# A row scale spread over the partitions through DRAM, and a first tile loaded in two halves, in a one-core encoder layer

## The chip, the cores and the metric

The kernel runs as one program on one core of a Trainium2 chip. The metric is the device time of an execution in microseconds. The profile is one execution taken by the hardware profiler; its engines are PE (TensorE matmul), PEld (TensorE weight loads), DVE (VectorE), ACT (ScalarE), POOL (GpSimd) and SP (SyncE, which issues most of the DMAs).

## The reference, cut to what matters

One layer of an encoder with two groups of heads side by side, on a prompt of 2048 tokens and a sample of 256, both with the same weights; then a gated MLP with a depthwise convolution over positions, and a final norm.

```python
def rmsnorm(x, w):
    y = x * lax.rsqrt(jnp.mean(x * x, axis=-1, keepdims=True) + EPS)
    return y * w

def encoder_layer(x, ...):
    h = rmsnorm(x, norm1_w)
    p = h @ w_in                                   # mLSTM q,k,v,o and gates; attention q,k,v
    mq, mk, mv, mo, gates, aq, ak, av = jnp.split(p, cuts, axis=-1)
    m_out = mlstm_mixer(mq, mk, mv, mo, gates, b_gates, mh_norm_w)   # both directions
    a_out = attention_mixer(aq, ak, av, q_norm_w, k_norm_w)          # 8 heads, 2 kv heads, rotary
    x = x + jnp.concatenate([m_out, a_out], axis=-1) @ w_out
    h = rmsnorm(x, norm2_w)
    u = centred_dwconv(h @ w_up, conv_w, conv_b)   # width 3 over positions
    a, g = jnp.split(u, 2, axis=-1)
    return x + (jax.nn.silu(g) * a) @ w_down
# then rmsnorm(x, final_norm_w); D_MODEL 1024, D_FF 2816, all float32
```

The change touches two places of this: the loading of the first tile of `x` for `h @ w_in`, and the scale `rsqrt(mean + EPS)` of the second norm, for one block of 256 tokens.

## The kernel before, in words

The 2304 tokens are 18 tiles of 128 (`NT`) or 9 blocks of 256 (`NB`, `BT`). Activations are kept transposed: the feature is the partition, tokens lie along the free dimension, and the 1024 features are eight chunks (`NCC`). Float32 products are made of three matmuls: each operand is split into a rounded part and the rest (`hi`, `lo`; ScalarE makes the first with a copy, VectorE the second with a subtraction), and hi·hi, hi·lo and lo·hi are added in PSUM.

The phases are: A, the norm-free projection of attention's columns and the gates; then the mLSTM and attention side by side (`run_both`); C, the output projection with the residual and the second norm; D, the MLP.

**Phase A's launch.** `front(i)` loads tile `i` of transposed `x` (512 KB, `g.xA[i]`) on SP's queue, and splits it into `nT`. `weights(cs)` loads chunk `c` of the weights (400 KB, `g.w_a[c]`) and splits it, scaled by the norm's weight, into `ws[c]` (helper `split`, L104 to L109). `mm` multiplies: the first call takes tiles 16 and 17 together, chunk by chunk, so that its first matmuls need only chunk 0 of the tile and of the weights. The program order is: tile 16 (the first of `order`), chunks 0 and 1 of the weights, tile 17, the other six chunks, tile 0, then the norms and the rotary tables (`tables`, `tables2`). `post1` turns a projected tile into q, k, v and gates, and frees one of three PSUM buffers `pj`.

**Phase C's tail.** Phase C goes over the nine blocks in the order `ORDER`, whose last is block 7. For each block `mm` (L989) projects into four PSUM tiles `po`; `post` adds the residual (L996), stores the new `x` to `x1_d` and squares it (L999); `tail` adds the squares up, gets the scale from `rstd_bc`, multiplies the four tiles `cx` by it and by the norm's weight (L1014, eight instructions) and stores them to `n2_d` (L1016; on POOL's queue for the last block, on SP's otherwise).

`rstd_bc` sums over partitions with matmuls against a matrix of ones (L128). The result is a column per 128 tokens: the token is the partition. From it comes the scale, for the last block (`act=True`) by a square root on ScalarE (L133), VectorE's reciprocal (L138) and a correction step in three VectorE instructions (L139 to L141), for all others by a power on POOL (L143). The multiplication in `tail` wants it the other way, along the free dimension and the same in every partition. L145 does that: for each 128 tokens a matmul whose stationary operand is the column repeated 128 times and whose moving operand is the identity. Its result stays in the same PSUM tile, `rs_c`.

For the last block the tail is called by `g.c_end()`, after the first two pairs of phase D's up-projection have been begun (tiles `pa`, `pb`) and their weight sums made (`sums`, L1110). Then phase C's pools are closed and phase D's opened over the same memory: the conv input tiles `u` (tag `u` of pool `d_s`, six buffers), the PSUM tiles `pc`, the conv outputs `y`, and three activation operands (`LATE`). The first `u` buffer lies over the bytes of phase C's `sq` and `rcol` buffers, another four over tiles of `cmx` that have been read out; the second `pc` bank is the bank of `rs_c`.

**Phase D** goes over three token blocks of 768 and eleven groups of the hidden dimension; each pair of 128 hidden columns is a Strassen-like product of seven multiplications (`11`, `21`, `t2`, `t1`, `t3`, `22`, `t4`) that share the banks `p1` (`pa`), `p2` (`pb`) and `p3` (`pc`). A step copies a bank to `u` on ScalarE (L1156) or adds it on VectorE (L1159) and then lets the next multiplication add into the bank (L1152). So the `t2` product of a pair, into `pa`, waits for the copy of `pa` into `u`; the `t1` product, into `pc`, waits for no copy.

**The order on each engine** is not the program's: a planner places instructions by priority, which is the place in the program (moved up within `tc.high_priority`), and by a simulation of when each is ready. It gives memory of closed pools to new tiles once the last users of the old ones are placed, and adds the waits that this needs, tile by tile. Each engine then executes its own list strictly in order.

Of the kernel before, what the change touches and what calls it, by code (L numbers as in the profile page):

```python
# [9 lines left out]
F32 = mybir.dt.float32  # L10
F32R = mybir.dt.float32r
AF = mybir.ActivationFunctionType
ALU = mybir.AluOpType
# [4 lines left out]
P = 128  # L18
D = 1024
NCC = D // P  # L20
# [65 lines left out]
def f32(ap):  # L86
    return ap.bitcast(F32)
# [14 lines left out]
def split(g, hi, lo, src, r, col=None):  # L102
    nc = g.nc
    nc.sync.dma_start(r, src)  # L104
    nc.scalar.activation(hi, r, AF.Copy, scale=1.0 if col is None else col)  # L105
    if col is None:
        nc.vector.tensor_tensor(lo, r, f32(hi), ALU.subtract)
    else:
        nc.vector.scalar_tensor_tensor(lo, r, col, f32(hi), ALU.mult, ALU.subtract)  # L109
# [10 lines left out]
def rstd_bc(g, sp, pp, sqs, n, ptag, name, bufs=1, act=False):  # L120


    nc = g.nc
    k = n // P
    ps = pp.tile([P, 512], F32, tag=ptag, name="rs_" + name, bufs=bufs)
    for t in range(k):
        for i, sq in enumerate(sqs):
            nc.tensor.matmul(ps[:, 504 + 2 * t:506 + 2 * t], sq[:, t * P:(t + 1) * P], g.ones, start=i == 0,  # L128
                             stop=i == len(sqs) - 1)
    r = sp.tile([P, 4], F32, tag="rcol", name="rcol_" + name)[:, 0:k]  # L130
    if act:
        sr = sp.tile([P, 4], F32, tag="rcol0", name="rcol0_" + name, bufs=1)[:, 0:k]
        nc.scalar.activation(sr, ps[:, 504:504 + 2 * k].rearrange("p (t o) -> p t o", o=2)[:, :, 0], AF.Sqrt, bias=g.eps)  # L133
    nc.vector.tensor_scalar(r, ps[:, 504:504 + 2 * k].rearrange("p (t o) -> p t o", o=2)[:, :, 0], EPS, None, ALU.add)
    if act:
        v, r = r, sr
        u = sp.tile([P, 4], F32, tag="rcol1", name="rcol1_" + name, bufs=1)[:, 0:k]
        nc.vector.reciprocal(r, r)  # L138
        nc.vector.scalar_tensor_tensor(u, r, -0.5, r, ALU.mult, ALU.mult)  # L139
        nc.vector.tensor_tensor(u, u, v, ALU.mult)  # L140
        nc.vector.scalar_tensor_tensor(r, u, 1.5, r, ALU.add, ALU.mult)  # L141
    else:
        nc.gpsimd.tensor_tensor(r, r, g.mhalf[:, 0:k], ALU.pow)  # L143
    for t in range(k):
        nc.tensor.matmul(ps[:, t * P:(t + 1) * P], r[:, t:t + 1].to_broadcast([P, P]), g.ident, start=True, stop=True)  # L145
    return ps[:, 0:n]


def phase_a(g, tc, sw, st_x, after_x, after_mm, after_pj):


    nc = g.nc
    with ExitStack() as st:
        sp = st.enter_context(tc.tile_pool(name="a_s", bufs=2, reuse_waits="tile"))
# [23 lines left out]
        def front(i):  # L178
            b, o = i // 2, i % 2
            nT = nTs[i] = sf.tile([P, NCC, 2, P], F32R, tag="nT", name=f"n1T{i}", bufs=3)  # L180
            n = order.index(i)
            x = xw[n] if n < NX0 else sx.tile([P, NCC, P], F32, tag="x", name=f"x{i}", bufs=3)
            nc.sync.dma_start(x, g.xA[i])
            nc.scalar.activation(nT[:, :, 0, :], x, AF.Copy)
            nc.vector.tensor_tensor(nT[:, :, 1, :], x, f32(nT[:, :, 0, :]), ALU.subtract)

        def norm(i):
            b, o = i // 2, i % 2
# [10 lines left out]
        def weights(cs):  # L199
            for c in cs:  # L200
                r = first[NX0 + c] if NX0 + c < 8 else sx.tile([P, D], F32, tag="x", name=f"ra{c}", bufs=3)
                split(g, ws[c][:, 0, :], ws[c][:, 1, :], g.w_a[c], r[:, 0:800], g.n1w[:, c:c + 1])
# [111 lines left out]
        def post2(i, kz):  # L314
# [5 lines left out]
            nc.scalar.dma_start(g.k_d[:, :, i * P:(i + 1) * P].rearrange("g p t -> p g t"), f32(kT))  # L320

        front(order[0])
        weights(range(0, 2))
        front(order[1])
        weights(range(2, NCC))
        front(order[2])
        for i in order[0:2]:
            norm(i)
# [616 lines left out]
def phase_c(g, sn, sp, pp, wps):  # L945
# [59 lines left out]
    def tail(b, x, acc):  # L1005
        if b == ORDER[-1]:
            sqs = [acc[:, 0], acc[:, 1], g.last_sq[:, 0], g.last_sq[:, 1]]
        else:
            nc.vector.tensor_tensor(acc[:, 0], acc[:, 0], acc[:, 1], ALU.add)
            sqs = [acc[:, 0]]  # L1010
        r = rstd_bc(g, sp, pp, sqs, BT, "r", f"c{b}", act=b == ORDER[-1])
        for z in range(4):
            for o in range(2):
                nc.vector.scalar_tensor_tensor(x[z][:, o], x[z][:, o], g.n2w[:, 2 * z + o:2 * z + o + 1],  # L1014
                                               r, ALU.mult, ALU.mult)
            (nc.gpsimd if b == ORDER[-1] else g.st).dma_start(g.n2_d[:, 2 * z:2 * z + 2, b * BT:(b + 1) * BT], x[z])  # L1016
        g.normed.add(b)
# [309 lines left out]
def down_phase(g, tc, st, s1, sl, banks):  # L1327
# [45 lines left out]
    def finish(accs, b, z, sms, bank):  # L1373
        r = rstd_bc(g, sp, bank, sms, H, "p", f"d{b}_{z}", bufs=4)

        def out(c):
            a = accs[c][:, Z[z]]
            if (b, z) == (ND - 1, 0) and c >= HALF:
                nc.vector.scalar_tensor_tensor(a, a, g.fw[:, c:c + 1], r, ALU.mult, ALU.mult)
            else:  # L1380
                nc.vector.tensor_tensor(a, a, r, ALU.mult)
            g.st.dma_start(g.yT[c, :, b * BLK + z * H:b * BLK + (z + 1) * H], a)
        for c in range(NCC):
            out(c)
# [55 lines left out]
def body(tc, aps, phases="abcd"):  # L1440
    nc = tc.nc
    g = Ctx()
# [3 lines left out]
    with ExitStack() as st:  # L1446
# [6 lines left out]
        def dram(name, shape):  # L1453
            setattr(g, name, dp.tile(shape, F32, name=name))
# [9 lines left out]
        dram("k_d", [2, P, T])  # L1464
        dram("v_d", [2, P, NT, 2, HD])
        dram("nm_d", [NT, 17, P])
        dram("og_d", [4, NB, P, 2, P])
        g.ident = kp.tile([P, P], F32, name="ident")
        make_identity(nc, g.ident)
# [12 lines left out]
        with ExitStack() as s2:  # L1482
# [8 lines left out]
            with ExitStack() as s3:  # L1491
                rp = pool(s3, "rowp", bufs=1)
                g.rows = rp.tile([40, 2, T], F32, name="rows")
                g.lnr = rp.tile([P, NT], F32, name="lnr")
                g.gtm = rp.tile([P, NT, 2, 16], F32, name="gtm")

                def after_x():
                    g.sn = pool(s_wo, "m_n", bufs=1, side="right")

                def after_mm():  # L1500
                    g.sm = pool(s_m, "m_s", bufs=2, side="right")

                def after_pj():
                    g.pj = pool(s_m, "m_j", bufs=MJ, space=PSUM, side="right")

                phase_a(g, tc, sw, s3.enter_context(ExitStack()), after_x, after_mm, after_pj)
                gate_math(g, tc)
# [143 lines left out]
```

## Time and profile before

| what | us |
|---|---|
| median of 3 runs (lowest, highest) | 3327.17 (3326.01, 3334.67) |
| the profiled execution | 3327.39 |
| its span, first to last instruction | 3325.7 |
| TensorE busy in the span | 3238.2 (97%) |
| VectorE busy | 2429.5 (73%) |
| ScalarE busy | 2002.8 (60%) |
| GpSimd busy | 519.0 (16%) |
| mean DMA rate | 184 GB/s |

Phase A takes the first 200 us or so, phase C's own blocks lie between about 1430 and 1850 us beside attention's last part, and phase D fills the rest. Line numbers in the profile (L145) are those of the kernel's file. A wait is shown as idle time before an instruction and, behind an arrow, the instruction whose semaphore ended it. Matmuls are pipelined: a matmul's duration is longer than the distance to the next, so the time of a row of matmuls is to be read from starts.

### The profile page before, as it was taken

Reading aid. Unit: us, or ns where it says so; the run is one execution under the profiler, and the core shown is the slowest. Engines: PE = TensorE matmul, PEld = TensorE weight load, DVE = VectorE, ACT = ScalarE, POOL = GpSimd, SP = SyncE. Lnnn points to the kernel's source line nnn. Section 1 sums busy time; section 2 is a strip of 40 time slices with the busy share of each in tenths; the row PEclk is TensorE's granted clock in tenths of the full one; section 3 lists DMA queues with packets and bytes.
Section 4 is the critical chain, followed back from the end, with each engine's and each line's share of the span. In section 5 each row is a group of like instructions: output and inputs, shape, how many; then the busy total and the mean of one; then the engine's idle time right before and its main releaser. Section 6 shows DMA issues by size and latency. Waiting matters only on the chain.

```text
span 3325.7 us, 53327 instructions
## 1 busy us (share of the span) xinstructions
PE 3238.2 (97%) x19488; PEld 3017.3 (91%) x19488; DVE 2429.5 (73%) x3768; ACT 2002.8 (60%) x3765; POOL 519.0 (16%) x916
## 2 busy tenths in 40 slices
PE   8989999999999999999999899999999999999998
PEld 7878888888888878878889899999999999999998
DVE  7855676676657778786665899998888888666664
ACT  5646666666675676665552655666666667554543
POOL 4551033222232322210000000000000000010101
PEclk9999999999999999999999899999999999999999
DMA  9973333332335433533227666668676557967663
GB/s 348 319 207 108 113 113 102 110 108 94 109 114 177 131 110 120 162 100 107 85 89 266 230 240 211 231 231 273 205 266 235 202 199 252 318 229 269 216 238 127
DMA packets 364301, 612.31 MB, mean 184 GB/s; under 512 B 31605, under 2 KB 220455, under 8 KB 364039
## 3 DMA queue, kind: packets, MB, share of 16 engines
q1 hardware_dynamic: 330727, 563.14, 50.4%
q0 software_dynamic: 11856, 33.96, 3.7%
q10 hardware_dynamic: 21456, 11.80, 1.2%
q8 instruction: 154, 2.52, 0.3%
q14 instruction: 108, 0.88, 0.1%
HBM read 444.85 MB, written 163.93 MB: 183 GB/s over the span
## 4 chain that ended last, share of the span: by engine, by line
PE 58%; issue 3%; DVE 2%; DMA 2%; ACT 2%; POOL 1%; SPq 0%; POOLq 0%; DVEq 0%; ACTq 0%
PE pa L1152 17%; PE pc L1152 8%; PE pf L1416 7%; PE po L989 5%; PE pb L1152 4%; PE ph L1416 4%; PE pg L1416 2%; PE ps L582 1%; PE mj L745 1%; PE ps L583 1%; PE pv L599 1%; PE pv L601 1%; PE pv L600 1%; PE px L559 1%; PE mv L745 1%
## 5 line engine op out<-in xcount | busy, mean ns | idle before, releaser
L588 DVE TENSOR_TENSOR xx<-pe,xx 128x1024 fp32r<-128x1024 f32 x260 | 318.8, 1227 | 128.1 <-ACT xx L587 126.5
L561 DVE TENSOR_REDUCE mx<-px 128x1 f32<-128x1024 f32 x256 | 310.8, 1217 | 100.2 <-PE px L559 99.1
L586 ACT ACTIVATE pe<-ps 128x1024 f32<-128x1024 f32 x260 | 266.4, 1025 | 171.0 <-PE ps L583 164.2
L587 ACT ACTIVATE xx<-pe 128x1024 fp32r<-128x1024 f32 x260 | 274.9, 1058 | 5.0
L1369 POOL TENSOR_TENSOR sq<-sq,sq 128x384 f32<-128x384 f32 x38 | 48.8, 1284 | 1377.9 <-ACT sq L1365 1294.9
L989 PEld LDWEIGHTS po<-cmx,wo 128*128 128x128 f32 x1728 | 227.2, 189 | 17.9 <-DVE cx L996 1.2
L989 PE MATMUL po<-cmx,wo 128*128 128x256 f32 x1728 | 234.6, 283 | 1.2 <-DVE cx L996 0.8
L1156 ACT ACTIVATE u<-pa 128x386 f32<-128x386 f32 (+2 forms) x264 | 129.1, 489 | 175.4 <-PE pa L1152 169.4
L601 PE MATMUL pv<-xx,vv 128*128 128x512 f32 x520 | 210.8, 405 | 7.4 <-DVE xx L588 7.3
L599 PE MATMUL pv<-xx,vv 128*128 128x512 f32 x520 | 211.5, 407 | 6.5 <-ACT rs L609 3.2
L582 PE MATMUL ps<-qq,kk 128*128 128x512 f32 x520 | 213.3, 410 | 3.1 <-DVE mx L561 1.5
L583 PE MATMUL ps<-qm,kl 65*128 65x512 f32 x520 | 208.6, 401 | 0.0
L600 PE MATMUL pv<-xx,vl 128*64 128x512 f32 x520 | 206.9, 398 | 0.0
L717 PEld LDWEIGHTS mj<-mn,wm 128*128 128x128 f32 x1296 | 177.6, 192 | 18.4 <-ACT og L733 4.1
L717 PE MATMUL mj<-mn,wm 128*128 128x256 f32 x1296 | 190.2, 287 | 3.3 <-ACT og L733 2.9
L727 PE MATMUL mv<-wm,mn 128*128 128x256 f32 x1296 | 188.6, 286 | 1.3 <-ACT qb L723 1.3
L727 PEld LDWEIGHTS mv<-wm,mn 128*128 128x128 f32 x1296 | 174.6, 190 | 14.0 <-ACT qb L723 2.3
L238 PE MATMUL pj<-w_a,n1T 128*128 128x512 f32 (+1 forms) x864 | 168.5, 354 | 10.0 <-ACT w_a L105 7.1
L238 PEld LDWEIGHTS pj<-w_a,n1T 128*128 128x128 f32 x864 | 141.8, 192 | 29.8 <-ACT w_a L105 7.1
L559 PE MATMUL px<-kk,qq 128*128 128x512 f32 x512 | 165.6, 404 | 2.8 <-ACT pe L586 2.5
L828 ACT ACTIVATE dm<-dm,tm 128x128 f32<-128x128 f32 x288 | 95.6, 392 | 101.1 <-POOL dm L825 97.1
L1152 PE MATMUL pc<-nt,wb 128*128 128x386 f32 (+2 forms) x792 | 147.2, 340 | 0.3 <-DVE cx L1014 0.3
(336 smaller groups left out, 8114.8 us busy)
## 6 DMA issues: line engine op xcount, KB each, us to landing
mn<-n_d SPq DMA_DIRECT2D x216, 256.0 KB, 3.1
ru<-w_up SPq DMA_DIRECT2D x88, 512.0 KB, 5.7
rs<-wsu_d SPq DMA_DIRECT2D x88, 512.0 KB, 5.7
act_d<-ts SPq DMA_DIRECT2D x33, 768.0 KB, 6.1
nt<-act_d SPq DMA_DIRECT2D x60, 384.0 KB, 4.6
re_t<-wsd_d SPq DMA_DIRECT2D x45, 512.0 KB, 5.4
wsu_d<-tw SPq DMA_DIRECT2D x44, 512.0 KB, 4.1
act_d<-ya SPq DMA_DIRECT2D x99, 192.0 KB, 2.9
```

The costliest lines, as they stand in the source:

```text
L238: nc.tensor.matmul(pjs[t][:, c0:c1], nTs[tiles[t]][:, c, a, :], ws[c][:, b, c0:c1], start=(c == 0 and k == 0), stop=(c == NCC - 1 and k == 2))
L561: nc.vector.tensor_reduce(s.mx[:, t0, z0:z0 + 1], ps, AX.X, ALU.max)
L582: nc.tensor.matmul(o, kk[:, kc:kc + P], s.qq, start=True, stop=False)
L586: nc.scalar.activation(pe, ps, AF.Exp)
L587: nc.scalar.activation(x[:, 0], pe, AF.Copy)
L588: nc.vector.tensor_tensor(x[:, 1], pe, f32(x[:, 0]), ALU.subtract)
L599: nc.tensor.matmul(s.pv, vv[:, kt % 4, :], x1, start=kt == 0, stop=False)
L717: nc.tensor.matmul(pj[:, o].rearrange("p (n t) -> p n t", t=P), s.w[c][:, a, o * P:(o + 1) * P], nT[c][:, :, h, :], start=(c + o + k == 0) ...
L727: nc.tensor.matmul(pv[:, o], nT[c][:, o, a, :], s.w[c][:, h, 256:512], start=(c + o + k == 0), stop=(c == NCC - 1 and k == 2 and o == 1))
L989: nc.tensor.matmul(po[:, o], wo[c][z // 2][:, a, n], mx[c][:, h, :], start=c + o + k == 0, stop=c == NCC - 1 and o == 1 and k == 2)
L1152: s.nc.tensor.matmul(p, w[:, aa, c, :], ops[k][:, c, bb, 0:s.n], start=c == 0 and i == 0 and not add, stop=c == NCC // 2 - 1 and i == 2, s ...
L1416: nc.tensor.matmul(ps[c], w[:, aa, c, :], t[:, gi - g0, bb, 0:H], start=gi == 0 and m == 0 and not more, stop=gi == NG - 1 and m == 2, ski ...
```

## The change

In `rstd_bc`, for the last block of phase C alone (`act=True`), the scale `r`, with the token as partition, is written by a DMA on POOL's queue to a small DRAM tensor `rl_d`, element by element in transposed order, and read back by another DMA on the same queue into a new SBUF tile `rb` with the row repeated in all 128 partitions. `rb` uses the one buffer of tag `sq`. The two matmuls of L145 are not issued for this block, and the eight multiplications of `tail` read `rb` from SBUF in place of `rs_c` from PSUM. The other blocks, and the final norm, are as before.

In `front`, the first tile of x is loaded in two DMAs of four chunks each, with a copy and a subtraction for each; the load and split of weight chunk 0 stand between the two halves in program order. `weights` is then called for chunk 1 alone behind it.

```diff
@@ rstd_bc
     else:
         nc.gpsimd.tensor_tensor(r, r, g.mhalf[:, 0:k], ALU.pow)
+    if act:
+        nc.gpsimd.dma_start(g.rl_d.rearrange("t p -> p t"), r)
+        rb = sp.tile([P, k, P], F32, tag="sq", name="rb_" + name, bufs=1)
+        nc.gpsimd.dma_start(rb, g.rl_d[:].unsqueeze(0).to_broadcast([P, k, P]))
+        return rb.rearrange("p t q -> p (t q)")
     for t in range(k):
         nc.tensor.matmul(ps[:, t * P:(t + 1) * P], r[:, t:t + 1].to_broadcast([P, P]), g.ident, start=True, stop=True)
     return ps[:, 0:n]
@@ phase_a, front
-            nc.sync.dma_start(x, g.xA[i])
-            nc.scalar.activation(nT[:, :, 0, :], x, AF.Copy)
-            nc.vector.tensor_tensor(nT[:, :, 1, :], x, f32(nT[:, :, 0, :]), ALU.subtract)
+            for c in (slice(0, NCC // 2), slice(NCC // 2, NCC)) if n == 0 else (slice(0, NCC),):
+                nc.sync.dma_start(x[:, c], g.xA[i, :, c])
+                if c.start == 0 and n == 0:
+                    weights(range(0, 1))
+                nc.scalar.activation(nT[:, c, 0, :], x[:, c], AF.Copy)
+                nc.vector.tensor_tensor(nT[:, c, 1, :], x[:, c], f32(nT[:, c, 0, :]), ALU.subtract)
@@ phase_a
         front(order[0])
-        weights(range(0, 2))
+        weights(range(1, 2))
         front(order[1])
@@ body
+        dram("rl_d", [2, P])
```

## The prediction

> **What bounds the kernel now.** I read the engine shares first, then TensorE's waits over the whole run, then order of time at the two places that the diff touches.
>
> The page's head: engine, busy time and share, instructions.
>
> ```profile
> span 3325.7 us, 53327 instructions
> PE 3238.2 (97%) x19488; PEld 3017.3 (91%) x19488; DVE 2429.5 (73%) x3768; ACT 2002.8 (60%) x3765; POOL 519.0 (16%) x916
> ```
>
> TensorE bounds it: 97% busy. So the question at each place is whether TensorE's idle time there shrinks or grows, and whether anything later takes that back. The view of waits, of 1780 to 1900 us and then from 1850 us to the end (total, times, longest):
>
> ```profile
> PE rs_c L145 <- DVE rcol_c L141: 15.2, 1, 15.2
> ...
> PE rs_d L128 <- POOL sq L1369: 4.5, 2, 4.3
> PE rs_d L145 <- POOL rcol_d L143: 1.2, 1, 1.2
> PE rs_d L128 <- DVE sq L1369: 1.1, 1, 1.1
> ```
>
> The first row is the longest single wait of TensorE that I found in the run, and the change removes the instruction that waits. The other three are all the waiting that follows 1850 us, 6.8 of 1475 us, each behind TensorE's own products: a shift of TensorE at 1850 us reaches the end in full. The timeline around the wait (start, duration, engine, line, operation, count, idle before):
>
> ```profile
> 1811.82 13.79 PE L989 MATMUL po<-cmx,wo 128*128 128x256 f32 x114
> ...
> 1828.03 0.59 PE L128 MATMUL rs_c<-ones,csq 128*128 128x2 f32 x4
> ...
> 1831.51 0.16 DVE L134 TENSOR_SCALAR rcol_c<-rs_c 128x2 f32<-128x2 f32 x1 [0.68 <-ACT rcol_c L133]
> ...
> 1832.25 0.95 DVE L1077 TENSOR_TENSOR nt<-nt 128x772 fp32r<-128x772 f32 x1
> ...
> 1834.93 1.22 DVE L1125 TENSOR_TENSOR wb<-tw,wb 128x1024 fp32r<-128x1024 f32 x1
> ...
> 1843.64 0.15 DVE L141 SCALAR_TENSOR_TENSOR rcol_c<-rcol_c,rcol_c 128x2 f32<-128x2 f32 x1
> 1843.85 1.22 PE L145 MATMUL rs_c<-ident,rcol_c 128*128 128x128 f32 x4 [15.23 <-DVE rcol_c L141]
> ...
> 1844.72 3.44 PE L1152 MATMUL pc<-nt,wb 128*128 128x386 f32 x12
> 1845.11 3.22 DVE L1014 SCALAR_TENSOR_TENSOR cx<-cx,nw,rs_c 128x256 f32<-128x256 f32 x8 [1.31 <-PE rs_c L145]
> 1845.24 0.88 ACT L1156 ACTIVATE u<-pa 128x386 f32<-128x386 f32 x2 [4.90 <-PE rs_c L145]
> ...
> 1848.47 2.34 PE L1152 MATMUL pc<-nt,wb 128*128 128x386 f32 x12 [0.31 <-DVE cx L1014]
> 1848.95 2.96 POOL L1016 DMA_DIRECT2D n_d<-cx  x4 [39.78 <-DVE u L1159]
> ...
> 1850.65 4.40 PE L1152 MATMUL pa<-nt,wb 128*128 128x386 f32 x24
> ```
>
> The reader is to see a chain: sums of squares (L128), four tiny DVE steps that stand between long DVE work and end at 1843.79, the spread (L145), eight multiplications (L1014), and behind them phase D. Two rows show how phase D hangs on it. ScalarE's first copy into `u` (L1156) waits for the spread: the first `u` buffer lies on the bytes of phase C's `sq` and `rcol` buffers, so it waits for their last reader. And the second `pc` product waits for the multiplications, since its PSUM bank is that of `rs_c`. The `pa` products at 1850.65 need that `u` copy, because they add into the bank that it empties.
>
> **The change part by part.** *The tail.* Removed: the two matmuls of L145 (four passes, 1.22 us). TensorE no longer waits for L141. The bank of `rs_c` now has its last reader at L134, over by 1831.67. So the two `pc` products (24 matmuls) follow L128 directly and need only `nt` (1833.20) and `wb`, the last of which is ready at 1836.15: they are done near 1842 even at a slow start. That empties the old place; it isn't yet a gain, for the next product in the order is the first `pa`, and it waits for the `u` copy.
>
> What that copy waits for has become longer. The new tile `rb` takes the one buffer of tag `sq`, under the first `u`; its last readers are the eight multiplications. New on the path are a POOL write of 256 single elements to DRAM and a POOL read of 128 KB that gives every partition the row. Neither shape is in the trace on POOL's queue; the nearest rows (landing times minimum, median, maximum; first POOL stores of `mix_d`, then SP reads of `rb` from `nm_d`, also a row of 256 elements for 128 partitions, then POOL reads of `dm` from `nm_d`, 256 KB to 128 partitions):
>
> ```profile
> L621 POOL DMA_DIRECT2D mix_d<-o x70: 521/550/623, 241.3 to 1723.8; - x70
> DMA to landing us min/median/max: 2.0/2.6/7.2
> ...
> L773 SPq DMA_DIRECT2D rb<-nm_d x9: 359/371/384, 1244.5 to 1402.1; - x9
> DMA to landing us min/median/max: 3.0/3.1/3.4
> ...
> L821 POOL DMA_DIRECT2D dm<-nm_d x72: 536/590/632, 234.9 to 1411.4; - x72
> DMA to landing us min/median/max: 3.3/3.7/6.9
> ```
>
> And how long POOL takes to begin after its data is made:
>
> ```profile
> 1722.27 0.41 DVE L615 TENSOR_TENSOR o<-o,rs 128x256 f32<-128x256 f32 x1
> ...
> 1723.21 1.08 POOL L621 DMA_DIRECT2D mix_d<-o  x2 [20.32 <-ACT xx L587]
> ```
>
> From 1722.68 to 1723.21 are 0.53 us. I take 0.53 + 2.6 for the write and 3.3 for the read: the SP row's 3.1, whose pattern is the same, and 0.2 for POOL's slower issue (590 against 371 ns). That is 6.4 us. The ends are 2.0 + 3.0 = 5.0 and 0.5 + 7.2 + 6.9 = 14.6.
>
> By "DMA: Bandwidth & Descriptors" of the Trainium skill, section on the anatomy of a SWDGE DMA, each such transfer costs about 2.0 us plus its bytes at 436 GB/s. By that, an estimate, the two take 2.0 + 2.3 = 4.3 us and the forecast falls by 2.1 us. The POOL rows here are longer (64 KB in 2.6 against its 2.15 us), so I keep the rows.
>
> Now the sum. The scale is ready at 1843.79 as before: L134 to L141 are untouched, and so is the DVE work between them. Plus 6.4 is 1850.2. The eight multiplications take 3.22 as before: 1853.4; from SBUF they may be a little shorter, at most 0.4 us. One `u` copy, half of 0.88 and a little overlap, is 0.5, and I allow 0.1 for handing over: TensorE starts the `pa` products near 1854.0, against 1850.65: **3.4 us later**.
>
> A second price comes with it. TensorE restarts slowly after a long idle time: twelve `pc` products took 3.44 us at 1844.72 and 2.34 at 1848.47; the four passes of L145 took 1.22 us, and in block 6:
>
> ```profile
> 1811.46 0.61 PE L145 MATMUL rs_c<-ident,rcol_c 128*128 128x128 f32 x4
> ```
>
> Together 1.1 + 0.6 = 1.7 us. Before, this lay under the wait for the multiplications; now TensorE idles from about 1842 to 1854 and pays it on products that the rest waits for. I add **1.7**; the ends are 0 and the 2.0 us that the launch shows below. Delay at the tail: **5.1 us**. The old path from 1843.79 to 1850.65 was 6.9 long, so the low end is 5.0 + 3.2 + 0.5 − 6.9 = 1.8, less 0.4 for SBUF, 1.4; the high end is 14.6 + 3.2 + 0.6 − 6.9 + 2.0 = 13.5.
>
> What else moves: on POOL's queue the four stores of `n2_d` (L1016) stand behind the two new DMAs and go some 5 us later. POOL had been idle for 39.8 us, so nothing else is delayed there; `n2_d` of block 7 is read only for the last third of phase D. The conv outputs' buffers wait for these stores too (L1273), but that work follows the pair's products, which move along by the same 5 us. SP issues the next `ru` loads after the `wd` split on DVE, also 5 us later; their weights are split before 1862.1 and used first at 1867.57:
>
> ```profile
> 1860.81 1.22 DVE L1125 TENSOR_TENSOR wa<-ru,wa 128x1024 fp32r<-128x1024 f32 x1
> ...
> 1867.57 4.42 PE L1152 MATMUL pa<-n,wa 128*128 128x386 f32 x24
> ```
>
> The use moves along, so 5 us of slack stay.
>
> *The launch.* Added: one DMA on SP, one ScalarE copy and one DVE subtraction, the copy and the subtraction each of half size, and the first weights' DMA before the second half of x. The rows:
>
> ```profile
> 5.05 1.06 ACT L184 ACTIVATE n1T<-first 128x1024 fp32r<-128x1024 f32 x1 [2.98 <-DMA first<-xA]
> ...
> 7.14 0.80 PE L238 MATMUL pj<-w_a,n1T 128*128 128x512 f32 x1 [7.14 <-ACT w_a L105]
> ...
> 26.96 1.26 DVE L216 COPY rot<-qkw 128x16 f32<-128x16 f32 x8 [7.78 <-DMA qkw<-q_norm_w]
> ...
> PE pj L238 <- DVE n1T L185: 1.9, 1, 1.9
> PE pj L238 <- DVE t L273: 0.5, 1, 0.5
> ...
> 10.00:15.00 5.00, 5.00 (x18) 4.26 (x17) 4.68 (x6) 4.62 (x6) 0.00 (x0) 1.00 1.03 396
> 15.00:20.00 5.00, 5.00 (x30) 4.42 (x29) 3.85 (x4) 3.67 (x5) 0.47 (x3) 1.00 1.06 395
> ...
> 30.00:35.00 5.00, 5.00 (x26) 4.18 (x25) 5.00 (x13) 3.25 (x5) 5.00 (x12) 1.00 1.02 347
> ```
>
> (The last three are stretches: length, busy time and count of PE, PEld, DVE, ACT, POOL; granted clock; DMA share; GB/s.) The first product can start earlier by at most the half copy (0.53) and the wait for half the tile, 256 KB at the 350 to 396 GB/s of these stretches, 0.7 us; I take 0.8 of these 1.2. But the stretches show TensorE slow at first (18 matmuls against 30 in 5 us, 2.0 us lost), and the two waits, at 38 and 40.6 us, 2.4 us together, end with DVE work. DVE is full from 30 us on, and its run began at 26.96 with a load that no part of the change brings earlier, since the DMA engines are full (share 1.03, 1.06). So TensorE's 0.8 us turn into a longer wait there: **0**, between −1.2 if DVE's order shifts with it and +0.4, one SP issue (371 ns in the row above) ahead of all later loads.
>
> **The rivals.** *The two transfers are slow.* The DMA engines are still full of weight traffic while the scale becomes ready:
>
> ```profile
> 1828.60:1844.00 15.40, 0.17 (x2) 0.15 (x1) 14.51 (x22) 11.33 (x14) 0.00 (x0) 0.55 1.04 369
> 1844.00:1851.00 7.00, 6.69 (x30) 6.39 (x31) 5.36 (x12) 2.56 (x6) 2.05 (x3) 0.78 0.30 105
> ```
>
> The share falls from 1.04 to 0.30 just then, which speaks against it; the 256 single elements, which no row shows, speak for it. At 14.6 us the delay is 11.5 and 1.7 for the restart: about 3340.6. It makes the kernel measurably slower (0.3%, 10 us, about what a measurement of this kernel can tell) once the two take 11.4 us.
>
> The same page of the Trainium skill says in its specifications that transfers under 512 B are done as read-modify-write; its rules call strided elements one descriptor each. By that the write is the suspect. No run here shows it yet.
>
> *TensorE finds other work in the gap.* The second pair's `u` buffers lie under `cmx` tiles that are read out by 1825.6, so that pair's products need not wait. If the planner orders them before the first pair's, TensorE does four more products (2.2 us each, half of 4.40) by 1854: 3.4 − 8.8 + 1.7 = −3.7, about 3323.5. Against it: the rows show both pairs' copies on ScalarE in program order, and phase D's buffers are handed out after the tail is placed.
>
> *The `pc` products stay behind the tail.* Then the old order holds and 4.7 us of work (twice 2.34) moves behind 1854: about 3337. Against it: nothing stands before them on TensorE once L145 is gone.
>
> *Nothing is felt.* Short transfers (5.0) and no slow restart: 1.4 us, with the launch's 1.2 gained, the time of before.
>
> **How the numbers follow.** The sum is made against the profiled execution, 3327.4 us (span 3325.7), which lies 0.2 us from the median of the runs. Plus 5.1 is 3332.5; its own range is 3329 to 3336. Chances: this 0.55; slow transfers 0.13; work in the gap 0.13; `pc` behind 0.05; nothing felt 0.14. A range of 3322 to 3338 leaves out most of the slow transfers and the far end of reordering elsewhere, since a planner that simulates the whole program may place other instructions anew. Over 0.3% slower: most of the slow transfers, some of `pc` behind, 0.14; over 0.3% faster needs nearly the whole 15.2 us, 0.06; within, 0.80.
>
> **What would show it.** Right: L145 gone for `rs_c` of block 7; twenty-four `pc` matmuls before 1843; then a gap of 10 us or more on TensorE that ends with the `u` copy, itself after L1014; the first `pa` 3 to 4 us later than 1850.65 and slow; at the launch an earlier first matmul and a longer wait near 38 to 41 us. Wrong: `pa` products of the second pair inside the gap, an earlier end of L141, or a write that lands after more than 5 us.

## The result: 23 us slower, and the profile after

The changed kernel takes 3351.24 us (median of 4 runs, 3350.45 to 3356.23) against 3328.45 us (4 runs, 3326.01 to 3334.67): a ratio of 1.0065, with a 95% interval of 1.0052 to 1.0077. The forecast was 3332.5 us, at most 3338. The mechanism came as forecast; two terms of its sum were far too small, and the launch wasn't free.

The head of the page after (span; engine, busy time and share, instructions):

```profile
span 3348.7 us, 53329 instructions
PE 3250.4 (97%) x19484; PEld 3026.4 (90%) x19484; DVE 2428.9 (73%) x3769; ACT 2002.8 (60%) x3766; POOL 519.1 (16%) x918
```

TensorE's waits after, from 1850 us to the end (total, times, longest):

```profile
PE pa L1160 <- ACT u L1164: 23.3, 1, 23.3
PE rs_d L128 <- POOL sq L1377: 4.3, 2, 2.8
PE rs_d L150 <- POOL rcol_d L143: 1.2, 1, 1.2
PE rs_d L128 <- DVE sq L1377: 1.1, 1, 1.1
```

The 15.2 us in front of the spread have gone, and 23.3 us in front of the first `pa` product have come. The timeline after, at that place (start, duration, engine, line, operation; line numbers are 5 to 8 higher than before):

```profile
1838.93 0.15 DVE L138 RECIPROCAL rcol_c<-rcol_c 128x2 f32<-128x2 f32 x1
...
1840.48 7.08 PE L1160 MATMUL pc<-nt,wb 128*128 128x386 f32 x24 [3.86 <-ACT wb L1132]
...
1850.98 0.15 DVE L141 SCALAR_TENSOR_TENSOR rcol_c<-rcol_c,rcol_c 128x2 f32<-128x2 f32 x1
1854.10 0.77 POOL L145 DMA_DIRECT2D rl_d<-rcol_c  x1 [37.52 <-issue]
1862.56 0.58 POOL L147 DMA_DIRECT2D rb_c<-rl_d  x1 [7.69 <-DMA rl_d<-rcol_c]
1866.92 3.26 DVE L1022 SCALAR_TENSOR_TENSOR cx<-cx,nw,rb_c 128x256 f32<-128x256 f32 x8 [15.79 <-DMA rb_c<-rl_d]
1868.10 3.11 POOL L1024 DMA_DIRECT2D n_d<-cx  x4 [4.96 <-DVE cx L1022]
1870.34 0.88 ACT L1164 ACTIVATE u<-pa 128x386 f32<-128x386 f32 x2 [22.64 <-DVE cx L1022]
...
1870.88 6.93 PE L1160 MATMUL pa<-nt,wb 128*128 128x386 f32 x24 [23.32 <-ACT u L1164]
```

Read it from the bottom: `pa` waits for the `u` copy, this for the multiplications (L1022), these for the read of `rb`, this for the write of `rl_d`, and this starts 2.97 us after L141 has ended at 1851.13. From L141's end to `pa` are 19.75 us, of which 15.8 lie in the write's start, its landing and the read. The stretch from 1854 to 1863 (length; busy time and count of PE, PEld, DVE, ACT, POOL; granted clock; DMA share; GB/s) shows that nothing competes:

```profile
1854.00:1863.00 9.00, 0.00 (x0) 0.00 (x0) 0.00 (x0) 0.00 (x0) 1.21 (x2) 0.50 0.01 0
```

The whole core stands still for one kilobyte, with the DMA engines at a share of 0.01. The DMA view of 1851 to 1871 us (KB each, us to landing):

```profile
rb_c<-rl_d POOLq DMA_DIRECT2D x1, 128.0 KB, 4.3
rl_d<-rcol_c POOLq DMA_DIRECT2D x1, 1.0 KB, 7.8
```

The difference of the two profiled spans, 23.0 us, splits at two marks. The reciprocal comes 7.3 us later (1838.93 against 1831.59). From there to the first `pa` product are 31.96 us against 19.06, 12.9 more, and from that product to the end 1477.8 against 1475.0, 2.8 more. The first says little of the change: among the experiments below whose launch is that of before, the reciprocal came at 1834.67 (`tail_only`) and at 1840.28 us (`tail_fixed`). The second proved the same wherever the tail is the same: 31.96 in `tail_only`, and 19.07 to 19.17 in three kernels with the tail of before. The third didn't: in `tail_only` the rest took 1474.0 us, less than before.

### The profile page after: what moved, and what is told of

It is laid out like the page before. It is cut to its first block, busy times and chain, and to the rows that moved or that the text cites. A ratio compares the mean times of both kernels' runs of the same rounds, so it can differ in the third digit from the quotient of the medians.

```text
span 3348.7 us, 53329 instructions
## 1 busy us (share of the span) xinstructions
PE 3250.4 (97%) x19484; PEld 3026.4 (90%) x19484; DVE 2428.9 (73%) x3769; ACT 2002.8 (60%) x3766; POOL 519.1 (16%) x918
## 4 chain that ended last, share of the span: by engine, by line
PE 82%; issue 6%; DMA 3%; DVE 3%; ACT 3%; POOL 2%; SPq 1%; POOLq 0%; ACTq 0%; DVEq 0%
PE pa L1160 17%; PE pc L1160 8%; PE pf L1424 7%; PE po L997 5%; PE pb L1160 4%; PE mj L725 4%; PE pj L246 4%; PE ph L1424 4%; PE mv L735 4%; PE ps L590 3%; PE pv L607 3%; PE ps L591 3%; PE pv L609 3%; PE pv L608 3%; PE px L567 3%
## 5 line engine op out<-in xcount | busy, mean ns | idle before, releaser
L246 PE MATMUL pj<-w_a,n1T 128*128 128x512 f32 (+1 forms) x864 | 169.1, 354 | 11.2 <-ACT w_a L105 6.9
L1160 PE MATMUL pa<-nt,wb 128*128 128x386 f32 (+2 forms) x792 | 147.9, 342 | 23.3 <-ACT u L1164 23.3
L1160 PEld LDWEIGHTS pa<-nt,wb 128*128 128x128 f32 x792 | 141.7, 191 | 23.6 <-ACT u L1164 23.6
```

The costliest lines, as they stand in the source:

```text
L246: nc.tensor.matmul(pjs[t][:, c0:c1], nTs[tiles[t]][:, c, a, :], ws[c][:, b, c0:c1], start=(c == 0 and k == 0), stop=(c == NCC - 1 and k == 2))
L1160: s.nc.tensor.matmul(p, w[:, aa, c, :], ops[k][:, c, bb, 0:s.n], start=c == 0 and i == 0 and not add, stop=c == NCC // 2 - 1 and i == 2, s ...
```

## The experiments

Ratios are to the kernel before on the same chip, where its median was 3330.8 to 3331.8. "Tail" is the spread through DRAM, "launch" the first tile's halves and the first weights.

### The two parts, each alone

`front_only`: the diff without its change in `rstd_bc` and without `rl_d`.

> Only the launch part of the change (first tile of x in two halves around the first weights); the tail is that of before. Theory A: the 7.3 us by which block 7's first DVE step (L134, 1831.51 before, 1838.85 after) came later were caused by the launch part, through the other order that the planner then wrote for DVE, ACT and POOL; then this kernel takes about 3327.4 + 5 to 8 = 3332 to 3335 us, and the shift of its TensorE is already 1 to 2 us at 90 us and 4 to 5 us at 1400 us. Rival (the prediction): the earlier start is absorbed at 40 us and nothing else moves: 3326 to 3328 us.

3336.3 us (12 runs), 1.0016 (1.0006 to 1.0026): about 5 us slower (2 to 9 by the interval), where I had forecast nothing. Behind the reciprocal its trace is that of before (1495.0 us to the end against 1494.1). TensorE's waits in its first 200 us, beside those of before (7.1 at first, 1.9 and 0.5 near 40 us, which the prediction shows, and 2.7 in three waits at the product now at L321):

```profile
PE pj L241 <- ACT w_a L105: 7.2, 1, 7.2
PE pj L241 <- ACT xh L251: 4.7, 1, 4.7
PE pk L321 <- DVE kz L286: 3.7, 1, 3.7
```

Single waits have grown and others have gone: all of TensorE's waits in the first 200 us add up to 16.3 us here, 15.0 before and 15.1 in the changed kernel. So they don't carry the 5 us.

`tail_only`: only the change in `rstd_bc`, and `rl_d`.

> Only the tail part (the scale of block 7 through DRAM); the launch is that of before. Theory: parts add up; the tail costs what lies between L134 and the first pa product (19.1 us before, 32.0 after, so 12.9) plus 2.8 behind it: 3343 us, with the same three long steps (POOL starts 3 us late, the write takes about 8 us to land, the read about 4). Rival: the POOL write was slow only because the launch part had shifted the weights' traffic against it; then it lands in 2.6 us as the prediction took, and the kernel takes about 3333 us.

3347.96 us (4 runs), 1.0052 (1.0034 to 1.0069). The order of all instructions is that of before up to the tail. From the reciprocal to the first `pa` are again 31.96 us. So the tail makes about 17 of the 23 us and the launch about 5; 0.52% and 0.16% make 0.68%, and 0.65% was measured for both.

### Which queue, and the buffer under `u`

`tail_sp`, and `tail_clear`, each against the tail alone:

```
tail_sp:    - nc.gpsimd.dma_start(g.rl_d..., r)    + nc.sync.dma_start(g.rl_d..., r)
            - nc.gpsimd.dma_start(rb, ...)         + nc.sync.dma_start(rb, ...)
tail_clear: - tag="sq", bufs=1 (rb), tag="rcol0", bufs=1 (root)   + tag="mx", bufs=MXB (both)
```

> As tail_only, but both new DMAs are issued on SP's queue. Theory W: the write of 256 single 4-byte elements to one KB of DRAM is slow whoever issues it; only POOL's late start (3.0 us) and its slower issue go, so the write still takes 6 us or more to land: about 3339 us. Rival Q: POOL's software queue made it slow; then the write lands in 2.2 us and the read in 3.1 as SP's other rows show, and the kernel takes about 3332 us.

3345.04 us, 1.0038 (1.0023 to 1.0053). SP's two transfers (start and landing):

```profile
L145 SPq DMA_DIRECT2D rl_d<-rcol_c x1: 370/370/370, 1847.8 to 1847.8; - x1
L147 SPq DMA_DIRECT2D rb_c<-rl_d x1: 319/319/319, 1855.4 to 1855.4; - x1
...
DMA to landing us min/median/max: 7.5/7.5/7.5
```

SP starts at once, and the write is as slow as POOL's. So the write is slow whoever issues it; POOL's late start is a term of its own.

> As tail_only, but the row tile rb and the column r lie in buffers of tag mx instead of sq and rcol0, so no longer under the first u buffer. Theory: the gap on TensorE is the wait of the u copy for the DRAM round trip through shared bytes; with other bytes the copy waits for L141 only, and the first pa product starts at about 1844.5 instead of 1863: TensorE's gap shrinks from over 20 us to about 4 us. What is late next are the stores of n2_d, for which the conv outputs wait: some of it may come back, so 3321 to 3333 us. Rival: something else in the tail holds phase D (the order on DVE, where L1014 stands before the u additions); then the gap and the time stay those of tail_only, about 3343 us.

3341.64 us, 1.0040 (1.0025 to 1.0056). The `u` copy comes right behind L141 and the first `pa` 12.9 us after the reciprocal, not 32: that `u` copy was indeed held by the bytes of `rb`. But of these 19 us few are kept: from the reciprocal to the end it took 1504.2 us, against 1506.0 for the tail alone. TensorE's waits from 1780 to 1900 us:

```profile
PE pa L1157 <- ACT u L1161: 8.0, 2, 4.3
PE pa L1157 <- DVE wd L1130: 5.3, 1, 5.3
PE pc L1157 <- ACT wb L1129: 3.9, 1, 3.9
```

The wait of 5.3 us is new: the split of `wd` stands behind the multiplications in VectorE's order, and these wait for `rb` as before.

### Why one kilobyte takes 8 us

Three layouts of the write, the rest of the tail unchanged:

```
tail_pairs:  rl_d [P, 2];     dma_start(g.rl_d[:], r)            128 pieces of 8 bytes
tail_spread: rl_d [2, P, P];  write to [..., 0]                  256 pieces of 4 bytes, 512 bytes apart
tail_lines:  rl_d [P, 2, 2];  write to [:, :, 0]                 256 pieces of 4 bytes, 8 bytes apart, by partition
```

> The tail alone, its DRAM rows laid out so that the write is 128 pieces of 8 bytes instead of 256 of 4 (same 1 KB, same queue; the scale factors come back in another order, which this kernel leaves so). In the tail alone the write landed 8.0 us after its start. Theory W (each small piece written into the same kilobyte costs some 20 to 30 ns one after another): the landing falls to about 2 + 128 x 0.024 = 5 us, TensorE's wait from 22.9 to about 20, the time by 3 us. Theory F (a fixed cost of a write to DRAM that a later transfer waits for): 8 us as before, time as the tail alone. The read stays at 4.2 us in both.

> The tail alone with still 256 pieces of 4 bytes, but each 512 bytes from the next (128 KB of DRAM, filled once at the start; the 1 KB that is read back is not the scale, which this kernel leaves so). Theory W2 (the pieces are slow because they share the same stretch of DRAM): the write lands in 2 to 3.5 us instead of 8.0 and the TensorE wait falls from 22.9 to about 17 to 18. Theory W1 (each piece under some size costs the same wherever it goes): about 8 us still. Two 64 KB stores more at the very start may move the rest of the program by a microsecond or two, so the verdict is read from the write's landing.

> The tail alone, its write still 256 pieces of 4 bytes, but laid out by partition with 4 bytes between them (2 KB in all; the kilobyte read back is not the whole scale, which this kernel leaves so). In the tail alone 32 bytes of every 64-byte stretch come from each of two groups of eight partitions; with 128 pieces of 8 bytes, and here, each group of eight partitions has its stretches for itself. Theory S (the write is slow, 8 us, where two DMA engines write into the same short stretch of DRAM): it lands in about 3.3 us, as with 128 pieces of 8 bytes (3.3) and with 512 bytes between pieces (3.1). Theory N (pieces of 4 bytes are slow within one or two kilobytes, pieces of 8 are not): about 8 us.

The three leave out putting the scale back in its place: `tail_pairs` reads it back in another order, the other two read a kilobyte of which only a part is the scale. They serve for times alone. What POOL's second transfer waits for in the three, in this order (one row of each kernel's view of `rl_d`: us, times):

```profile
  POOL rb_c L147: 3.3, 1
```

```profile
  POOL rb_c L147: 3.1, 1
```

```profile
  POOL rb_c L147: 3.8, 1
```

It was 7.9 for the tail alone. Halving the number of pieces would have given 5 by the first theory; 3.3 refutes a price for each piece, and 256 pieces of 4 bytes in 3.1 and 3.8 us refute a price for small pieces as such. What the slow layout alone has is that neighbours in one short stretch of DRAM come from different groups of partitions; by the theory, different DMA engines write them. That theory passed all three, but no view shows which DMA engine wrote which piece, and the size of the stretch wasn't measured. One rival isn't quite out: the two layouts by partition also put half as many pieces into a short stretch as the slow one does. If the delay went with that number, about half of the 4.8 us between 7.9 and 3.1 should have stayed; 0.2 and 0.7 did. The times are 3342.64 (1.0040), 3341.16 (1.0032) and, one run, 3343.16 us: 5 to 7 us better than the tail alone. With so few runs the intervals overlap that of the tail alone, and in the traces most of what is won at the first `pa` is gone by the end (1504.5, 1504.0 and 1506.2 us from the reciprocal, against 1506.0).

"DMA: Bandwidth & Descriptors" of the Trainium skill states in its specifications that transfers under 512 B are done as read-modify-write. All four layouts have pieces under that size, and three are quick: so the size alone doesn't make a write slow here.

### Why POOL starts 3 us late

`tail_warm`: in `rstd_bc`, `nc.gpsimd.dma_start(g.rw_d[:], v)` ahead of the reciprocal.

> The tail alone with one more small POOL DMA (256 x 4 bytes into a DRAM array of its own) issued when the mean squares are ready, about 12 us before the real write. Theory P (POOL's first DMA after a pause of over 100 us starts about 3 us late, the next ones 0.5 us after their data): the dummy starts about 3 us after its data, the real write starts 0.4 to 0.8 us after L141 instead of 2.97, and the first pa product comes 2.4 us sooner (29.5 us after the reciprocal instead of 31.96). Theory Q (the write itself, with its many pieces, takes POOL 3 us to prepare): 2.97 us as before.

```profile
1837.35 0.16 DVE L134 TENSOR_SCALAR rcol_c<-rs_c 128x2 f32<-128x2 f32 x1 [0.65 <-ACT rcol_c L133]
1840.47 0.59 POOL L138 DMA_DIRECT2D rw_d<-rcol_c  x1 [25.43 <-DVE tw L1116]
...
1849.48 0.15 DVE L142 SCALAR_TENSOR_TENSOR rcol_c<-rcol_c,rcol_c 128x2 f32<-128x2 f32 x1
1849.95 0.74 POOL L146 DMA_DIRECT2D rl_d<-rcol_c  x1 [8.88 <-DVE rcol_c L142]
```

The dummy bears the 3 us (1837.51 to 1840.47) and the real write starts 0.32 us after its data, as theory P said; the first `pa` comes 2.9 us sooner. The time is no better, 3349.28 us (1.0055, 1.0041 to 1.0069): the write still lands after 8.0 us, and in the profiled execution more than the 2.9 us is lost later (TensorE's waits for POOL's squares in the final norm are 8.8 us, 2.3 in `tail_only`).

The dummy's own landing matters too. It has the quick layout of `tail_pairs`, 128 pieces of 8 bytes by partition, and yet it took 9.1 us (KB, us to landing):

```profile
rw_d<-rcol_c POOLq DMA_DIRECT2D x1, 1.0 KB, 9.1
```

While it was under way, from 1840.4 to 1849.7 us, the DMA share was 1.03; it was 0.01 during the write of `tail_pairs`. The traffic is the likely reason, though no run tested it. So a quick layout alone doesn't make a small write quick.

But P's reason, the pause, then fell by two traces made for another purpose. `tail_spread` and `tail_lines` have two stores and one store of 128 rows more at the very start, on POOL. There the write starts 0.3 us after L141 in both with the same pause, and an earlier store is late instead. `tail_lines`, with 128 rows more (the store before the write):

```profile
1722.62 0.41 DVE L620 TENSOR_TENSOR o<-o,rs 128x256 f32<-128x256 f32 x1
1726.21 1.09 POOL L626 DMA_DIRECT2D mix_d<-o  x2 [22.96 <-issue]
```

and `tail_spread`, with 256 rows more (a pair of stores earlier still):

```profile
1676.91 0.43 DVE L620 TENSOR_TENSOR o<-o,rs 128x256 f32<-128x256 f32 x1
1680.49 1.09 POOL L626 DMA_DIRECT2D mix_d<-o  x2 [21.91 <-issue]
```

Both start 3.2 us after their data, where the last one of before took 0.53. A `mix_d` store writes 64 rows, and they come in twos: each 128 rows added at the start move the late place by just two stores of 64 rows. So it belongs to a count of rows that have gone through POOL's queue, not to a pause. It isn't a count of DMAs, since one DMA more would have moved it by one store, nor of bytes, since `tail_lines` adds 2 KB and `tail_spread` 128. The kernel before has it too, at the first `n2_d` store (1848.95, where the first multiplications end at 1845.98), and it cost nothing there. The kernels `tail_sp`, `tail_fixed` and the three `chain` kernels below have it at the same store, 2.97 us in each. What ends after that count no run shows.

### All faults of the tail mended

`tail_fixed`: pairs of 8 bytes, read back through a strided view; both transfers on SP; `rb` and the root in tag `mx`.

> The tail alone with all three faults mended that the runs so far point to: the write laid out as 128 pieces of 8 bytes (the multiplications read the factors back through a strided view, so the values are those of the kernel before), both transfers issued by SP, and rb and the root in a tag that lies clear of u. From L141: write issued at once, landed after 3.3, read 3.9, multiplications start about 7.3 us after L141 instead of 15.8. Theory W+U (slow write and the buffer under u are the tail's whole cost): TensorE's waits of 5.3 and 3.7 us behind it vanish, reciprocal to end 1494 to 1497 (1494.1 before, 1506.0 for the tail alone), 3329 to 3334 and a ratio of 0.999 to 1.001. Rival R (two DMA latencies cost in themselves): the wait for wd behind the multiplications stays at 3 us or more and the ratio is 1.002 or above.

3335.41 us (11 runs), 1.0008 (1.0000 to 1.0017), and 1497.0 us from the reciprocal to the end. So the write, POOL and the buffer together were nearly the whole cost: of 0.52% some 0.1% is left. The expected way to it was wrong, though: TensorE's waits didn't vanish, one of 8.2 us took their place. The chain behind it (start, length, what):

```profile
1852.52 4.36 DMA rl_d<-rcol_c
1856.88 0.02 issue
1856.90 3.85 DMA rb_c<-rl_d
1860.75 0.03 issue
1860.77 3.26 DVE cx L1020 x8
1864.03 0.94 DVE u L1165 x2
1864.97 0.61 DVE wd L1131
1865.58 0.02 issue
1865.59 4.54 DMA ru<-w_up
```

The multiplications hold VectorE's order, behind them the split of `wd`, which frees a `ru` buffer, whose load the next weights wait for. The multiplications end 23.8 us after the reciprocal against 16.7 before, and that comes back on TensorE 25 us after the first `pa`.

### What the 15.2 us of before were

All three keep the spread by TensorE and change only the steps ahead of it:

```
chain_pow:       - act=b == ORDER[-1]   + act=False      (POOL's power operation, as in the other blocks)
chain_pow_moved:   the same, three gpsimd.memset of [P, 1] at the start, g.c_end() at high priority
chain_short:     - L139, L140, L141                      (the reciprocal goes to the spread as it is)
```

> The kernel before, with its spread by TensorE kept and only the way to the scale of the last block changed: the square root, reciprocal and three small VectorE steps (12.2 us, because long VectorE work stands between them) replaced by the one POOL power operation that all other blocks use (0.71 us). Theory: what held TensorE 15.2 us was this chain, not the spread (1.2 us): the spread comes 8 to 11 us sooner, TensorE's wait falls to about 4 to 7 us, and part of it is given back at the next waits for u and wd, so 3320 to 3325 (ratio 0.997 to 0.999). Rival: all of it is given back behind the tail, as most of the 20 us of the kernel with rb clear of u were: 3328 to 3332.

3331.03 us (11 runs), 0.9998 (0.9988 to 1.0008): no gain. TensorE's wait for the spread did fall from 15.2 to 6.6 us, as the theory said. But the first `pa` came 19.0 us after L134, as before (19.1): 4.4 us came back where the second `pc` product waits for the last multiplications, and 2.1 us in slower `pc` products (7.9 us for the 24, against 5.8). So it ended as the rival said. The timeline:

```profile
1837.19 0.15 DVE L134 TENSOR_SCALAR rcol_c<-rs_c 128x2 f32<-128x2 f32 x1
1837.42 5.69 POOL L143 TENSOR_TENSOR rcol_c<-rcol_c,mhalf 128x2 f32<-128x2 f32 x1 [20.61 <-DVE rcol_c L134]
1840.20 2.36 DVE L1125 TENSOR_TENSOR wb<-tw,wb 128x1024 fp32r<-128x1024 f32 x2
1843.16 0.93 PEld L145 LDWEIGHTS rs_c<-ident,rcol_c 128*128 128x128 f32 x4 [6.72 <-POOL rcol_c L143]
```

POOL's operation took 5.69 us, where it takes 0.71 in the other eight blocks.

> The kernel before with POOL's power operation for the last block's scale (in the run before it took 5.69 us there, 0.71 in the other blocks), and with three small POOL fills more at the start, which move POOL's program on by three instructions; the tail is given a higher priority. Theory C (the 3 to 5 us that POOL loses here belong to one place in its program, instruction 1256 or 1257, and not to a pause or to the operation): the power operation takes 0.7 us, TensorE's wait for the spread falls from 6.63 to about 1.7 us, and the time to 3325 to 3328 (0.998 to 0.999), less what comes back at the next wait (4.44, for the multiplications that read the same PSUM bank). Theory D (it belongs to the operation among VectorE's long work there): 5.7 us again, 3331 us again.

3327.40 us (11 runs), 0.9982 (0.9973 to 0.9990): the one version that is measurably quicker than the kernel before. But the theory behind it fell:

```profile
L143 POOL TENSOR_TENSOR rcol_c<-rcol_c,mhalf x9: 692/716/5687, 1516.1 to 1830.6; 128x2 f32<-128x2 f32 x9
```

5.69 us again, at another place of POOL's program, as theory D said. From L134 to the end are 1493.7 us in both kernels (1494.1 before), so in these executions the gain doesn't come from the tail; it lies ahead of it, and which of the edits makes it stays open.

> The kernel before with its TensorE spread, and the refinement between reciprocal and spread left out: the factor is the reciprocal of ScalarE's square root as it is, so three of four VectorE steps (L139, L140, L141) are gone and with them the 12.2 us between reciprocal and L141. Theory K (the 15.2 us that TensorE waits in the kernel before are this chain, the spread itself is 1.2): the spread ends within 2 us of the reciprocal and TensorE's wait falls from 15.2 to 3 to 5 us (until the first wb split); of the 10 to 12 us some 4 to 8 come back where the second pc product waits for the last multiplication, which reads the same PSUM bank: 3323 to 3328, ratio 0.997 to 0.999. Rival: all comes back there, 3329 to 3332.

3326.98 us (12 runs), 0.9991 (0.9980 to 1.0002): likely a small gain, not secured. The trace shows the mechanism. TensorE's waits from 1780 to 1900 us:

```profile
PE pc L1148 <- DVE cx L1010: 5.7, 1, 5.7
PE rs_c L141 <- DVE rcol_c L137: 3.1, 1, 3.1
```

The spread starts 0.2 us after the reciprocal and TensorE's wait is 3.1 us instead of 15.2: the wait was the chain's, and the spread costs its 1.2 us. Of the 12 us, 5.7 come back at once where the second `pc` product waits for its PSUM bank, and 1488.5 us from the reciprocal to the end against 1494.1 leave 5.5 in this execution.

### Which half of the launch

`front_halves`: two halves of the tile, weights where they were. `front_weights`: tile whole, first weights ahead of it.

> The launch alone, and of it only the two halves: first tile of x loaded and split in two halves, both ahead of all weights. The launch of the change cost 5.3 us (1.0016, interval 1.0006 to 1.0026). Theory H (the two more instructions shift the planned order of the first 200 us, with gaps of 4.7 us near 40 us and 3.7 near 184 us, each over the 3.4 us behind which the granted clock drops): here the planned order shifts too, so the cost stays, 3334 to 3338. Theory X (what costs is the weights between the halves): 3329 to 3332, first matmul within 0.3 us of 7.14.

> The launch alone, and of it only the order: first tile of x whole, but the first weights loaded and split ahead of it. Planned orders differ in nothing else. Theory H: no shift of the planned order, so no cost beyond the launch itself, first matmul within 1 us of 7.14, 3329 to 3333. Theory X: the cost of the launch of the change, about 5 us, is here.

3334.36 us (12 runs), 1.0003 (0.9992 to 1.0014), and 3335.05 us (12 runs), 1.0005 (0.9997 to 1.0014). Neither is told from no change, and neither interval excludes half of the 0.16%. Both started TensorE later than before (7.6 and 8.0 us against 7.1), and the two together not (7.2). Theories H and X both stay open.

## Why the prediction was wrong, step by step

- *TensorE goes on with both `pc` products:* right. They ran from 1840.48 to 1847.56, at a mean granted clock of 0.65.
- *The next is the first `pa`, behind the `u` copy, behind the multiplications:* right, and shown by `tail_clear`, where that wait goes. No product of the second pair came into the gap.
- *POOL begins 0.53 us after its data:* 2.97, so 2.4 us short. The price lay in the trace: the first `n2_d` store of before began 2.97 us after the first two multiplications, and I read only the start of the last `mix_d` store.
- *The write takes 2.6 us:* 8.5 from start to start of the read, 5.9 short. This is the step that failed, by the prediction's own sign too (a write that lands after more than 5 us). I took the row of a store with 64 long rows for one of 256 single elements, and gave the unlike shape only the far end of the bound.
- *The read takes 3.3 us:* 4.4, 1.1 short.
- *Multiplications and `u` copy:* 3.26 and 0.7 against 3.22 and 0.6. Read from SBUF the multiplications were no shorter; no run shows the 0.4 us that I allowed for that at the low end.
- Together 19.75 us against 10.25, so the first `pa` came 12.9 us later and not 3.4: the difference of 9.5 is the sum of these terms.
- *Restart at the slow clock:* right in kind. The first 24 `pa` products took 6.93 us against 4.40 before, 2.5 more where I had 1.7 (in `tail_only` 5.84, 1.4 more). With the 12.9 us the delay is 15.4 (14.3 in `tail_only`), above even the high bound of 13.5.
- *A shift of TensorE at 1850 us reaches the end in full:* about so where the first `pa` is late, with 1477.8 and (`tail_only`) 1474.0 us from it to the end, against 1475.0 before. Not where it is early: 1491.3 in `tail_clear`, 1484.1 in `tail_fixed`, since VectorE's order holds the next weights.
- *The rival of slow transfers* (chance 0.13, deciding from 11.4 us, 3340.6 at 14.6): this is what happened, with 15.8 us for the two. The DMA share that I held against it, falling from 1.04 to 0.30, had nothing to do with it here: the write was slow with the engines empty (0.01).
- *Launch at 0 (−1.2 to +0.4):* about 5 us. The first matmul of the changed kernel came at 6.86, 0.28 us earlier, not 0.8, since ScalarE had to wait for the first weights. The wait near 40 us grew as said, but by more (first rows of TensorE's waits in the first 60 us, after):

```profile
PE pj L246 <- ACT w_a L105: 6.9, 1, 6.9
PE pj L246 <- ACT xh L256: 4.0, 1, 4.0
```

The two more instructions also changed the planner's order of the first 200 us, which I had named and not priced. But all waits of these 60 us are 11.2 against 9.9 us, and of the first 200 us 15.1 against 15.0, so the waits don't make the 5 us. Nor does the granted clock show it. From 1400 to 1500 us, where the order of work is the same, it was 1.00 before and 0.97 after; but in `tail_only`, whose launch is that of before, it was 0.97 too (the rows of before, of after and of `tail_only`).

```profile
1400.00:1500.00 100.00, 92.97 (x531) 74.98 (x530) 82.32 (x147) 65.89 (x120) 13.08 (x24) 1.00 0.34 109
```

```profile
1400.00:1500.00 100.00, 93.34 (x511) 75.09 (x510) 81.82 (x147) 66.68 (x129) 12.27 (x24) 0.97 0.34 109
```

```profile
1400.00:1500.00 100.00, 93.08 (x521) 76.26 (x520) 81.14 (x145) 64.40 (x118) 11.58 (x22) 0.97 0.33 105
```

So that stretch isn't the launch's doing. The launch's 5 us rest on times alone (those of `front_only`, and of the whole change against its tail), and where in the program they arise stays open.

## What to carry to other kernels

A wait of an engine isn't the price of the instruction that waits: ask first what is late, and here it was a chain of four tiny steps (12.2 us) that the change left in place, not the spread (1.2 us). Before a value is sent through DRAM, price the exact shape of the write: lay it out so that each partition's pieces stand together, and let its landing buffers lie clear of whatever the next stage fills first. And when a transfer's shape isn't in the trace, its far bound deserves more than the chance left over.

## What the runs showed of the hardware

- A write of 1 KB in 256 pieces of 4 bytes, interleaved over the partitions, landed after 7.5 us from SP (DMA share 0.20) and 7.8 to 8.4 from POOL (0.01 to 0.24). Laid out by partition or with 512 bytes between the pieces it took 3.2 to 3.9 from POOL (0.01 to 0.27) and 4.4 from SP (0.26). With the DMA engines full (1.03) a write laid out by partition took 9.1.
- One of POOL's DMAs starts 2.97 to 3.2 us after its data instead of 0.3 to 0.5, after a certain count of rows, whatever the pause before it.
- POOL's power operation on 128x2 values took 5.69 us beside back-to-back operations of VectorE, and ended 0.55 us after the last of them (1842.56 to 1843.11); 0.71 us where VectorE was idle. "GPSIMD Engine Reference" of the Trainium skill, section Specifications, says that POOL's SBUF interfaces are shared with VectorE and contended where its instructions have two SBUF inputs. These rows agree; no run took VectorE's work away to prove it. What started first seems to count: in `chain_pow` a power on 128x3 values that began at 3137.49, 0.08 us ahead of a VectorE operation with two inputs, took 0.86 us, as with VectorE idle; one that began at 2967.53, 0.15 us behind such an operation, took 1.82.
